# Weight remainders, softmax row maxima and gate functions on other engines, in a two-group encoder layer on Trainium2

## The chip, the cores and the metric

The kernel runs on one core of one Trainium2 chip. Five engines of that core work beside each other, each with its own instruction stream that it takes in order: TensorE (PE, matrix products; PEld is its loading of the stationary operand), VectorE (DVE), ScalarE (ACT), GpSimd (POOL) and SyncE (SP), which here issues every DMA. Matrix products land in PSUM banks, which have to be emptied by VectorE or ScalarE before they can be used again. The metric is the device time of one execution in microseconds; lower is better.

## The reference

One encoder layer is applied to two request groups (1024 tokens by 1024 channels each, float32) that share all weights:

```
mod = silu(c) @ w_ada + b_ada             -> shift, scale, gate
h   = rms_norm(x, norm_g) * (1 + scale) + shift
qa, ka, va, za, qb, kb, vb, zb, ga, gb = split(h @ w_in)
oa  = gqa_attention(rope(rms(qa)), rope(rms(ka)), va) * silu(za)
ob  = rms_norm(diff_attention(...qb, kb, vb, lam), subln_g) * (1 - lam_init) * silu(zb)
merged = sigmoid(ga) * (oa @ w_proj_a) + sigmoid(gb) * (ob @ w_proj_b)
y   = x + gate * (merged @ w_out)
```

Branch A has 8 query heads and 2 key heads of 64; branch B has 4 heads, each with two softmax maps of 1024 by 1024 whose weighted difference is applied to the values. za and zb go through SiLU, ga and gb through a sigmoid.

## The kernel before

**Arithmetic.** Most products are made in three passes: each float32 operand is split into a rounded part (format fp32r) and a remainder, and the products high by high, high by low and low by high are added in one PSUM bank. The rounded part is an ACT copy, the remainder a subtraction. `load_w` (L188) fetches a weight block of 1024 by 256 in four staging tiles `st` (three buffers); `split_w` (L176) rounds each on ACT (L179) and subtracts on POOL, or, in the stages where `alone[0]` is true, on DVE for every second tile (L181). `load_w_proj` (L215) does the same for the two projection matrices, always on POOL (L223).

**One group.** `head` projects keys, values and the first queries of branch A (`kva_gen`, `qa_gen`). Then six attention phases follow, one for each half of A's heads and one for each head of B (`attention`, L869). A step of `scores` (L743) calls `softmax_unit` (L727): four products fill a two-bank score tile `s` (two such tiles exist), DVE reduces the row maximum (L736) and multiplies it by the row's scale `rs`, a column of 128 numbers (L737), and ACT takes the exponential with that scale and bias (L738) into a tile `p` (four buffers). `flip` transposes `p` on DVE in blocks of 32 (L771) and four DMAs put it into `q` (L776); ACT and DVE split it (L784, L785) and PE multiplies by the values (L796, L797, or L836 for B).

**Filling.** PE is kept busy between attention steps by projections for the next phase (L514) and by "z pieces" (`z_gen`, L692). There are 48 of them for each group: 12 blocks of 256 columns (za, zb, then ga and gb by turns), four pieces each. A piece is 24 products into one bank (L703), which ACT copies into the single tile `ev` (L709) and a DMA stores to DRAM (L712). For the first two blocks (za; `SILU = 2`) that copy is a SiLU; the other blocks are stored raw. How many pieces lie in the head and in each phase stands in `Z_HEAD` and `Z_SHARE` (their sixth number is not used); the rest goes into the last phase. How the streams are interleaved is set by `weave` (L72) from `ATT_W`, `IN_A` and `Z_A`, by numbers set by hand.

**End of a group.** `gated_gen` (L909) reads attention outputs and z back from DRAM, takes SiLU of z where it was stored raw (L931), multiplies (L936 for A, L942 for B, then L946 by the row factors) and splits (L947, L948). `merge_gen` (L953) projects each branch (L976), reads a pair of ga or gb tiles into `gg` (L966), takes their sigmoid on ACT (L967, 128 by 1024), and DVE multiplies the product in PSUM by it (L987 for A, L982 for B, which then adds A's part, L983). 16 of these merge pieces belong to A, `16 - TAIL` of them run beside the last attention phase. `out_gen` is the output projection (L1005, L1010).

**Order on the engines.** The program order comes from `weave`. The tile framework then orders each engine's instructions by a simulated timeline with priorities; attention steps are issued at high priority (L886). Every DMA is issued in order on SP.

**At the start**, `start` (L339) makes SiLU of the conditioning vector (L340), and products with `w_ada` make shift and scale; `gate_gen` (L445) makes the gate later.

Of the kernel before, what the change touches and what calls it, by code (L numbers as in the profile page):

```python
# [12 lines left out]
F32 = mybir.dt.float32  # L13
F32R = mybir.dt.float32r
AF = mybir.ActivationFunctionType
ALU = mybir.AluOpType
# [9 lines left out]
HD = 64  # L26
# [5 lines left out]
C_GA, C_GB = 3328, 4352  # L32
# [2 lines left out]


Z_SHARE = (
    (7, 19, 5, 3, 3, 4),
    (9, 14, 7, 3, 2, 6),
)  # L40
Z_HEAD = (6, 6)
Z_HEAD_A = (-0.4, -0.45)
ATT_W = (
    (1.07, 0.837, 1.1, 0.95, 1.07, 1.52),
    (1.15, 1.354, 1.035, 1.15, 0.85, 1.069),
)
IN_A = (
    (0.1, 0.05, 0.2, 0.05, 0.15, 0.1),
    (0.1, -0.05, 0.45, 0.15, 0.15, 0.65),
)  # L50
Z_A = (
    (0.1, 0.0, 0.4, 0.0, 0.0, 0.0),
    (0.15, 0.05, 0.35, 0.15, -0.1, -0.1),
)
LAST_ATT, LAST_FILL = (44, 26)
GATED_A = -0.3
TAIL = 6
TAIL_A = 0.3
LAG = 2

SILU = 2

CUTS = (3, 6)

# [26 lines left out]
def kernel(ctx: ExitStack, tc: tile.TileContext, t: dict):  # L91
    nc = tc.nc
# [83 lines left out]
    def split_w(w, q, st):  # L176
        wh = w[:, q * 2 : q * 2 + 2, 0, :]
        wl = w[:, q * 2 : q * 2 + 2, 1, :]
        nc.scalar.activation(wh, st, AF.Copy)  # L179
        e = nc.vector if alone[0] and q % 2 else nc.gpsimd  # L180
        e.tensor_tensor(out=wl, in0=st, in1=wh.bitcast(F32), op=ALU.subtract)  # L181

    def split_early(what):
        w, sts = what
# [30 lines left out]
    def load_w_proj(br, half):  # L215

        w = wpool.tile([P, 4, 2, 512], F32R, tag="w", name=nm("w"))
        mat = t["w_proj_b" if br else "w_proj_a"][0]
        for c in range(4):
            st = spool.tile([P, 512], F32, tag="st", name=nm("st"))  # L220
            dma(st, mat[c * P : (c + 1) * P, half * 512 : (half + 1) * 512])
            nc.scalar.activation(w[:, c, 0, :], st, AF.Copy)
            nc.gpsimd.tensor_tensor(out=w[:, c, 1, :], in0=st, in1=w[:, c, 0, :].bitcast(F32), op=ALU.subtract)  # L223
        return w


# [183 lines left out]
    def load_tables_B():  # L410
        for dst, src in ((cosB, "cosB"), (sinB, "sinB")):
            for a in range(2):
                dma(dst[:, a], t[src].rearrange("(n p) d -> p n d", p=P))
        for i, src in enumerate(("qn_b", "kn_b")):
            dma(gB[:, i, :], t[src][0].partition_broadcast(P))
        nc.vector.tensor_scalar(out=gB[:, 0, :], in0=gB[:, 0, :], scalar1=SC, scalar2=None, op0=ALU.mult)
        for a in range(2):
            by_q(cosB[:, a], sinB[:, a], gB[:, a], 8)

        nc.vector.tensor_tensor(out=gB[:, 0, 16:], in0=gB[:, 0, 16:], in1=gB[:, 1, 16:], op=ALU.mult)  # L420

# [12 lines left out]
        dma(subg, t["subln_g"].rearrange("o e -> e o"))  # L434
        nc.vector.tensor_scalar(out=subg, in0=subg, scalar1=(1.0 - LAM_INIT) * math.sqrt(2 * HD), scalar2=None, op0=ALU.mult)

    def load_tables_A(st):

# [6 lines left out]
    def gate_gen():  # L445
        for half in range(2):
            acc = gbank()[:2]
            for k in range(NCH):
                st = spool.tile([P, 512], F32, tag="st", name=nm("st"))
                col = 2 * D + half * 512  # L450
                dma(st, w_ada[k * P : (k + 1) * P, col : col + 512])
                nc.tensor.matmul(acc, cT[:, k], st, start=(k == 0), stop=(k == NCH - 1))
                if k % 2:
                    yield 1
            row = rtile()[:2]
            nc.vector.tensor_copy(row, acc)
            ps = gbank()[:, :8].rearrange("p (c g) -> p c g", g=2)
            for c in range(4):
                nc.tensor.transpose(ps[:, c, :], row[:, c * P : (c + 1) * P], ident[:2, :2])
            cs = slice(half * 4, half * 4 + 4)  # L460
            nc.vector.tensor_tensor(
                out=gatec[:, cs], in0=ps, in1=bcol[:, 2, cs].unsqueeze(2).to_broadcast([P, 4, 2]), op=ALU.add
            )


    def ht_gen(g, ht):
# [222 lines left out]
            yield 1  # L689


    def z_gen(ht, col, dst, i0, fn=AF.Copy):  # L692
        w = load_w(w_cols(w_in, (col, 256)))
        for hf in range(2):
            for e in range(2):
# [10 lines left out]
                        )  # L706
                        k += 1
                ev = mtile("ev", [P, 512], bufs=1)
                nc.scalar.activation(ev, ps, fn)  # L709
# [17 lines left out]
    def softmax_unit(q, rs, sw, k, pt, su):  # L727
# [6 lines left out]
            nc.tensor.matmul(s[:, sl], q, k[:, sl], start=True, stop=False)  # L734
            nc.tensor.matmul(s[:, sl], sw, k[:, sl], start=False, stop=True)  # L735
        nc.vector.tensor_reduce(out=m, in_=s, axis=AX.X, op=ALU.max, negate=True)  # L736
        nc.vector.tensor_tensor(out=m, in0=m, in1=rs, op=ALU.mult)  # L737
        nc.scalar.activation(  # L738
            pt.rearrange("p (j c a) -> p j c a", j=4, c=8), s.rearrange("p (c a j) -> p j c a", c=8, j=4),
            AF.Exp, scale=rs, bias=m, accum_out=su,  # L740
# [168 lines left out]
    def gated_gen(st, i, hf, oT):  # L909

        if i == 0 and hf == 0:
            su = st["suA"].rearrange("p j n -> p (j n)")
            nc.vector.reciprocal(su, su)
            ps = fbank()[:64, :P]
            nc.tensor.transpose(ps, su, ident)
            row = rtile()[:64, :P]
            nc.scalar.activation(row, ps, AF.Copy)
            dma(st["rA"], row)
        rA = st["rA"].rearrange("(j h n) p -> j h (n p)", j=8, h=2)
        u = utile().rearrange("p (c s n) -> p c s n", c=2, s=2)  # L920
# [4 lines left out]
        for c in range(2):  # L925
# [1 line left out]
            o, z = (os_[c], zs_[c]) if i == 3 else (rtile(), rtile())  # L927
            dma(o, st["od"][e][hf])
            dma(z, st["zd"][(e, hf)])
            if i >= SILU:  # L930
                nc.scalar.activation(z, z, AF.Silu)  # L931
            if e < 4:
                rb = mtile("tab", [P, 512])
                for a in range(2):
# [18 lines left out]
    def merge_gen(st, br, oT, mT):  # L953

        for half in range(2):
            w = load_w_proj(br, half)
            for hf in range(2):
# [3 lines left out]
                for d in range(4):  # L961
                    dt_ = half * 4 + d
                    if d % 2 == 0:
                        gg = ptile().rearrange("p (a n) -> p a n", a=2)
                        for a in range(2):
                            dma(gg[:, a, :], st["gbd" if br else "gad"][(dt_ + a, hf)])  # L966
                        nc.scalar.activation(gg, gg, AF.Sigmoid)  # L967
                        if br:
                            mT[hf].append(utile().rearrange("p (c s n) -> p c s n", c=2, s=2))
                    g = gg[:, d % 2, :]  # L970
# [8 lines left out]
                            k += 1  # L979
                    if br:  # L980
                        mh, ml = (mT[hf][dt_ // 2][:, d % 2, i, :] for i in range(2))
                        nc.vector.tensor_tensor(out=g, in0=ps, in1=g, op=ALU.mult)  # L982
                        nc.vector.tensor_tensor(out=g, in0=g, in1=md[:, d], op=ALU.add)  # L983
                        nc.scalar.activation(mh, g, AF.Copy)
                        nc.vector.tensor_tensor(out=ml, in0=g, in1=mh.bitcast(F32), op=ALU.subtract)
                    else:
                        nc.vector.tensor_tensor(out=md[:, d], in0=ps, in1=g, op=ALU.mult)  # L987
                    yield 1

    def out_gen(g, mT):  # L990
# [95 lines left out]

    def z_item(st, i):
        ht = st["ht"]
        fn = AF.Silu if i < SILU else AF.Copy
        if i < 2:  # L1090
            return z_gen(ht, C_ZA + i * 256, st["zd"], i * 2, fn)
        if i < 4:
            return z_gen(ht, C_ZB + (i - 2) * 256, st["zd"], i * 2, fn)
        i -= 4
        if i % 2 == 0:
            return z_gen(ht, C_GA + i * 128, st["gad"], i)
        return z_gen(ht, C_GB + (i - 1) * 128, st["gbd"], i - 1)

    states = [new_state(0), new_state(1)]
    late = start(states[0]["ht"])  # L1100
# [111 lines left out]
```

## Time and profile before

| | |
|---|---|
| time, median of 3 runs | 1973.39 us (1972.16 to 1973.81) |
| span of the profiled execution, first to last instruction | 1971.9 us |
| TensorE (PE) busy | 1901.8 us, 96% |
| weight loads (PEld) busy, beside PE | 1619.1 us, 82% |
| VectorE (DVE) busy | 1353.0 us, 69% |
| ScalarE (ACT) busy | 1012.0 us, 51% |
| GpSimd (POOL) busy | 680.9 us, 35% |
| data moved by DMA | 295 MB, 150 GB/s on average |

The profiled execution has no time of its own beside its span. The three timed runs lie 0.3 to 1.9 us above that span, the median 1.5 us; that is what lies around it. A row of a group of instructions reads: line, engine, operation, out<-in with the program's tile names (buffer numbers left out), shapes, count, then busy time and the mean duration in ns, then the idle time of that engine just before, and what ended it. A row of waits reads: who waited <- for whom: total us, how many times, longest. A row of the timeline begins with start and duration in us, and ends, in brackets, with the idle time before it. A row of windows gives the busy time of each engine in a stretch, its granted TensorE clock and its share of DMA time.

### The profile page before, as it was taken

How to read it: one execution, taken by the hardware profiler on the slowest of the kernel's cores; microseconds unless marked ns; L12 is line 12 of the kernel's file. 1: busy time of each engine (PE TensorE's matmuls, PEld its weight loads, DVE VectorE, ACT ScalarE, POOL GpSimd, SP SyncE). 2: the span in 40 equal slices, each digit the busy share in tenths (PEclk: the TensorE clock that was granted, in tenths of full speed). 3: DMA queues.
4: the chain of work that ended last, by engine and by line, in shares of the span. 5: the costliest groups of instructions: out<-in, count | busy, mean ns of one | idle time of the engine just before them, and what ended most of it. 6: DMA issues, size and time to landing. Idle time of an engine off the chain costs nothing. (4 is left out here: it accounts for less than half of the span.)

```text
span 1971.9 us, 30870 instructions
## 1 busy us (share of the span) xinstructions
PE 1901.8 (96%) x10466; PEld 1619.1 (82%) x10466; DVE 1353.0 (69%) x2165; ACT 1012.0 (51%) x1920; POOL 680.9 (35%) x958
## 2 busy tenths in 40 slices
PE   8999999999989999999999999999999999998999
PEld 3888888888878985778889788888888889776887
DVE  4658876786888577757465598768878766776641
ACT  4447655565655353464323576556666444447410
POOL 2363511442446251322235344114444426322210
PEclk9899999999999999999999999999999999999999
DMA  9125545556454345865641355555555334478431
GB/s 315 33 89 149 144 139 149 158 156 174 127 144 111 89 117 173 272 234 179 222 151 44 115 144 167 148 149 157 156 152 161 98 102 119 120 222 267 166 102 75
DMA packets 271614, 295.26 MB, mean 150 GB/s; under 512 B 37856, under 2 KB 220256, under 8 KB 271456
## 3 DMA queue, kind: packets, MB, share of 16 engines
q1 hardware_dynamic: 271456, 293.28, 50.1%
q8 instruction: 84, 1.38, 0.3%
q14 instruction: 74, 0.61, 0.1%
HBM read 133.72 MB, written 42.01 MB: 89 GB/s over the span
## 5 line engine op out<-in xcount | busy, mean ns | idle before, releaser
L703 PE MATMUL f<-u,w 128*128 128x512 f32 x2184 | 561.3, 395 | 3.0 <-ACT w L179 1.3
L514 PE MATMUL f<-w,u 128*128 128x256 f32 x3456 | 489.6, 286 | 5.2 <-ACT ev L709 2.7
L514 PEld LDWEIGHTS f<-w,u 128*128 128x128 f32 x3456 | 460.7, 192 | 26.8 <-ACT ev L709 3.7
L703 PEld LDWEIGHTS f<-u,w 128*128 128x128 f32 x2184 | 396.8, 189 | 78.1 <-ACT w L179 1.8
L181 POOL TENSOR_TENSOR w<-st,w 128x512 fp32r<-128x512 f32 x166 | 227.8, 1391 | 463.2 <-ACT w L179 412.9
L736 DVE TENSOR_REDUCE m<-s 128x1 f32<-128x1024 f32 x256 | 310.2, 1217 | 55.1 <-PE s L735 52.0
L771 DVE STREAM_TRANSPOSE p<-p 128x1024 f32<-128x1024 f32 x192 | 238.0, 1241 | 112.8 <-ACT p L738 110.2
L785 DVE TENSOR_TENSOR q<-q,hi 128x512 fp32r<-128x512 f32 x256 | 193.9, 774 | 47.9 <-ACT hi L784 46.4
L738 ACT ACTIVATE p<-s,m,rsB 128x1024 f32<-128x1024 f32 x128 | 154.0, 1204 | 135.0 <-DVE m L737 103.3
L738 ACT ACTIVATE p<-s,m,rsA 128x1024 f32<-128x1024 f32 x128 | 153.8, 1202 | 128.1 <-DMA q<-p 95.8
L735 PE MATMUL s<-u,sw 128*128 128x512 f32 x512 | 205.0, 401 | 0.0
L784 ACT ACTIVATE hi<-q 128x512 fp32r<-128x512 f32 x256 | 153.2, 624 | 78.2 <-DMA q<-p 50.2
L179 ACT ACTIVATE w<-st 128x512 fp32r<-128x512 f32 x196 | 114.2, 626 | 101.9 <-DMA st<-in_w_in_dram 46.6
L976 PE MATMUL f<-u,w 128*128 128x512 f32 x552 | 136.4, 400 | 11.3 <-ACT ev L709 4.1
L796 PE MATMUL a<-hi,u 128*128 128x256 f32 x512 | 132.0, 284 | 4.8 <-DVE oo L813 3.1
L976 PEld LDWEIGHTS f<-u,w 128*128 128x128 f32 x552 | 104.8, 192 | 35.3 <-DVE u L987 4.6
L836 PE MATMUL a<-q,u 128*128 128x256 f32 x512 | 125.9, 385 | 5.6 <-DMA q<-p 1.9
L797 PE MATMUL a<-q,u 128*128 128x256 f32 x512 | 129.8, 287 | 0.5 <-DVE q L785 0.4
L734 PE MATMUL s<-u 128*128 128x512 f32 x256 | 109.5, 428 | 7.9 <-ACT p L738 4.0
L734 PE MATMUL s<-u,u 128*128 128x512 f32 x256 | 103.3, 404 | 13.8 <-ACT p L738 9.0
L836 PEld LDWEIGHTS a<-q,u 128*128 128x128 f32 x512 | 95.9, 193 | 21.6 <-issue 2.9
L735 PEld LDWEIGHTS s<-u,sw 128*128 128x128 f32 x512 | 97.4, 190 | 15.5
(186 smaller groups left out, 2639.1 us busy)
## 6 DMA issues: line engine op xcount, KB each, us to landing
q<-p SPq DMA_DIRECT2D x768, 128.0 KB, 2.6
st<-in_w_in_dram SPq DMA_DIRECT2D x132, 256.0 KB, 3.0
zd<-ev SPq DMA_DIRECT2D x96, 256.0 KB, 2.2
sw<-u SPq DMA_DIRECT2D x256, 64.0 KB, 2.0
p<-zd SPq DMA_DIRECT2D x64, 256.0 KB, 3.8
u<-in_w_ada_dram SPq DMA_DIRECT2D x8, 1024.0 KB, 10.4
st<-in_w_in_dram SPq DMA_DIRECT2D x64, 128.0 KB, 2.7
st<-in_w_out_dram SPq DMA_DIRECT2D x32, 256.0 KB, 3.2
```

Source lines behind the costliest of these rows:

```text
L181: e.tensor_tensor(out=wl, in0=st, in1=wh.bitcast(F32), op=ALU.subtract)
L514: nc.tensor.matmul(ps, lt[c][:, sl], w[:, c, wi, :], start=(k == 0), stop=(k == 23))
L703: nc.tensor.matmul(ps, w[:, c, wi, e * P : (e + 1) * P], rt[c], start=(k == 0), stop=(k == 23),)
L734: nc.tensor.matmul(s[:, sl], q, k[:, sl], start=True, stop=False)
L735: nc.tensor.matmul(s[:, sl], sw, k[:, sl], start=False, stop=True)
L736: nc.vector.tensor_reduce(out=m, in_=s, axis=AX.X, op=ALU.max, negate=True)
L738: nc.scalar.activation(pt.rearrange("p (j c a) -> p j c a", j=4, c=8), s.rearrange("p (c a j) -> p j c a", c=8, j=4), AF.Exp, scale=rs, bi ...
L771: nc.vector.transpose(pt, pt)
L784: nc.scalar.activation(th, tl.bitcast(F32), AF.Copy)
L785: nc.vector.tensor_tensor(out=tl, in0=tl.bitcast(F32), in1=th.bitcast(F32), op=ALU.subtract)
L836: nc.tensor.matmul(acc, u["v"][:, k], pT[:, k], start=(k == 0), stop=(k == 7))
L976: nc.tensor.matmul(ps, w[:, c, wi, d * P : (d + 1) * P], o[:, oi, :], start=(k == 0), stop=(k == 11))
```

## The change

- **Weight remainders:** all of them are subtracted by DVE instead of POOL (`split_w`, `load_w_proj`).
- **Row maxima:** the multiplication of the row maximum by the row scale becomes an ACT copy with a scale.
- **Gates:** SiLU and sigmoid are written with tanh: sigmoid(x) = (1 + tanh(x/2)) / 2. The factors 1/2 go into constants: into `subg` for B, into the row factors (L917) for A, into `gatec` for the merge. Each z piece is emptied by a tanh; for za and zb, DVE then makes (1 + tanh) times the bank and writes `ev`. The SiLU of `gated_gen` and the sigmoid of `merge_gen` go; DVE's multiplications in the merge become (1 + g) times the bank. The conditioning vector's SiLU is made the same way.
- **Pieces:** numbers of `Z_SHARE`, `Z_HEAD`, `ATT_W`, `IN_A`, `Z_A` and `TAIL` are changed.

```
-    (7, 19, 5, 3, 3, 4),
+    (7, 19, 6, 3, 2, 4),
     (9, 14, 7, 3, 2, 6),
-Z_HEAD = (6, 6)
+Z_HEAD = (6, 5)
 ATT_W = (
-    (1.07, 0.837, 1.1, 0.95, 1.07, 1.52),
-    (1.15, 1.354, 1.035, 1.15, 0.85, 1.069),
+    (1.07, 0.933, 1.1, 0.95, 1.129, 1.52),
+    (1.15, 1.354, 1.035, 1.196, 0.85, 1.069),
 IN_A = (
-    (0.1, 0.05, 0.2, 0.05, 0.15, 0.1),
-    (0.1, -0.05, 0.45, 0.15, 0.15, 0.65),
+    (0.1, -0.05, 0.2, 0.05, 0.15, 0.1),
+    (0.1, -0.05, 0.45, 0.25, 0.15, 0.65),
 Z_A = (
-    (0.1, 0.0, 0.4, 0.0, 0.0, 0.0),
-    (0.15, 0.05, 0.35, 0.15, -0.1, -0.1),
+    (0.1, 0.0, 0.4, -0.05, -0.2, 0.0),
+    (0.15, 0.05, 0.35, 0.15, -0.3, -0.2),
-TAIL = 6
+TAIL = 5
-SILU = 2
...
     def split_w(w, q, st):
         nc.scalar.activation(wh, st, AF.Copy)
-        e = nc.vector if alone[0] and q % 2 else nc.gpsimd
-        e.tensor_tensor(out=wl, in0=st, in1=wh.bitcast(F32), op=ALU.subtract)
+        nc.vector.tensor_tensor(out=wl, in0=st, in1=wh.bitcast(F32), op=ALU.subtract)
...
     def load_w_proj(br, half):
-            nc.gpsimd.tensor_tensor(out=w[:, c, 1, :], in0=st, in1=w[:, c, 0, :].bitcast(F32), op=ALU.subtract)
+            nc.vector.tensor_tensor(out=w[:, c, 1, :], in0=st, in1=w[:, c, 0, :].bitcast(F32), op=ALU.subtract)
...
     def start(ht):
-        nc.scalar.activation(cT, ccol, AF.Silu)
+        nc.scalar.activation(cT, ccol, AF.Tanh, scale=0.5)
+        nc.vector.scalar_tensor_tensor(out=cT, in0=cT, scalar=1.0, in1=ccol, op0=ALU.add, op1=ALU.mult)
+        nc.vector.tensor_scalar(out=cT, in0=cT, scalar1=0.5, scalar2=None, op0=ALU.mult)
...
     def gate_gen():
+            nc.vector.tensor_scalar(out=gatec[:, cs], in0=gatec[:, cs], scalar1=0.5, scalar2=None, op0=ALU.mult)
...
     def z_gen(ht, col, dst, i0, gated):
                 ev = mtile("ev", [P, 512], bufs=1)
-                nc.scalar.activation(ev, ps, fn)
+                nc.scalar.activation(ev, ps, AF.Tanh, scale=0.5)
+                if gated:
+                    nc.vector.scalar_tensor_tensor(out=ev, in0=ev, scalar=1.0, in1=ps, op0=ALU.add, op1=ALU.mult)
...
     def softmax_unit(q, rs, sw, k, pt, su):
-        nc.vector.tensor_tensor(out=m, in0=m, in1=rs, op=ALU.mult)
+        nc.scalar.activation(m, m, AF.Copy, scale=rs)
...
     def gated_gen(st, i, hf, oT):
-            nc.scalar.activation(row, ps, AF.Copy)
+            nc.scalar.activation(row, ps, AF.Copy, scale=0.5)
...
-            if i >= SILU:
-                nc.scalar.activation(z, z, AF.Silu)
...
     def merge_gen(st, br, oT, mT):
-                        nc.scalar.activation(gg, gg, AF.Sigmoid)
...
-                        nc.vector.tensor_tensor(out=g, in0=ps, in1=g, op=ALU.mult)
+                        nc.vector.scalar_tensor_tensor(out=g, in0=g, scalar=1.0, in1=ps, op0=ALU.add, op1=ALU.mult)
...
-                        nc.vector.tensor_tensor(out=md[:, d], in0=ps, in1=g, op=ALU.mult)
+                        nc.vector.scalar_tensor_tensor(
+                            out=md[:, d], in0=g, scalar=1.0, in1=ps, op0=ALU.add, op1=ALU.mult
+                        )
```

More of the change, by code (lines that the diff above doesn't have):

```diff
@@ L37 @@
 Z_SHARE = (
-    (7, 19, 5, 3, 3, 4),
+    (7, 19, 6, 3, 2, 4),
     (9, 14, 7, 3, 2, 6),
 )
-Z_HEAD = (6, 6)
+Z_HEAD = (6, 5)
 Z_HEAD_A = (-0.4, -0.45)
 ATT_W = (
-    (1.07, 0.837, 1.1, 0.95, 1.07, 1.52),
-    (1.15, 1.354, 1.035, 1.15, 0.85, 1.069),
+    (1.07, 0.933, 1.1, 0.95, 1.129, 1.52),
+    (1.15, 1.354, 1.035, 1.196, 0.85, 1.069),
 )
 IN_A = (
-    (0.1, 0.05, 0.2, 0.05, 0.15, 0.1),
-    (0.1, -0.05, 0.45, 0.15, 0.15, 0.65),
+    (0.1, -0.05, 0.2, 0.05, 0.15, 0.1),
+    (0.1, -0.05, 0.45, 0.25, 0.15, 0.65),
 )
 Z_A = (
-    (0.1, 0.0, 0.4, 0.0, 0.0, 0.0),
-    (0.15, 0.05, 0.35, 0.15, -0.1, -0.1),
-)
-LAST_ATT, LAST_FILL = (44, 26)
+    (0.1, 0.0, 0.4, -0.05, -0.2, 0.0),
+    (0.15, 0.05, 0.35, 0.15, -0.3, -0.2),
+)
+LAST_ATT = 44
+LAST_FILL = 26
 GATED_A = -0.3
-TAIL = 6
+TAIL = 5
 TAIL_A = 0.3
 LAG = 2
-SILU = 2
 CUTS = (3, 6)
@@ L434, in load_tables_B @@
         dma(subg, t["subln_g"].rearrange("o e -> e o"))
-        nc.vector.tensor_scalar(out=subg, in0=subg, scalar1=(1.0 - LAM_INIT) * math.sqrt(2 * HD), scalar2=None, op0=ALU.mult)
+        nc.vector.tensor_scalar(out=subg, in0=subg, scalar1=0.5 * (1.0 - LAM_INIT) * math.sqrt(2 * HD), scalar2=None, op0=ALU.mult)
     def load_tables_A(st):
@@ L689, in vb_gen, with z_gen @@
             yield 1
-    def z_gen(ht, col, dst, i0, fn=AF.Copy):
+    def z_gen(ht, col, dst, i0, gated):
         w = load_w(w_cols(w_in, (col, 256)))
@@ L1088, in z_item @@
         ht = st["ht"]
-        fn = AF.Silu if i < SILU else AF.Copy
         if i < 2:
-            return z_gen(ht, C_ZA + i * 256, st["zd"], i * 2, fn)
+            return z_gen(ht, C_ZA + i * 256, st["zd"], i * 2, True)
         if i < 4:
-            return z_gen(ht, C_ZB + (i - 2) * 256, st["zd"], i * 2, fn)
+            return z_gen(ht, C_ZB + (i - 2) * 256, st["zd"], i * 2, True)
         i -= 4
         if i % 2 == 0:
-            return z_gen(ht, C_GA + i * 128, st["gad"], i)
-        return z_gen(ht, C_GB + (i - 1) * 128, st["gbd"], i - 1)
+            return z_gen(ht, C_GA + i * 128, st["gad"], i, False)
+        return z_gen(ht, C_GB + (i - 1) * 128, st["gbd"], i - 1, False)
     states = [new_state(0), new_state(1)]
```

## The prediction

> **What bounds the kernel now.** I read the page's first part, then the busy times by stretch, then what TensorE waited for, and last the timeline at its longest waits.
>
> ```profile
> PE 1901.8 (96%) x10466; PEld 1619.1 (82%) x10466; DVE 1353.0 (69%) x2165; ACT 1012.0 (51%) x1920; POOL 680.9 (35%) x958
> ```
>
> TensorE is the bound: all that a change which leaves its products alone can win is its idle time, 1971.9 - 1901.8 = 70 us, and what its clock loses. The change has the same products, so the question is only which of these stalls go and which come.
>
> ```profile
> core 0: us, PE busy (x) PEld busy (x) DVE busy (x) ACT busy (x) POOL busy (x), PEclk, DMA share, GB/s
> ...
> 1095.00:1150.00 55.00, 50.17 (x258) 41.71 (x256) 34.99 (x47) 35.93 (x58) 18.73 (x20) 0.97 0.51 145
> 820.00:850.00 30.00, 25.89 (x112) 21.25 (x113) 19.55 (x29) 18.59 (x27) 6.69 (x9) 0.94 0.93 298
> 1775.00:1805.00 30.00, 23.07 (x98) 17.72 (x97) 22.60 (x36) 22.39 (x27) 4.50 (x6) 0.94 0.86 283
> 150.00:820.00 670.00, 650.82 (x3734) 559.08 (x3733) 501.76 (x768) 372.70 (x719) 249.34 (x374) 0.99 0.52 147
> ```
>
> The first three rows are the second group's first softmaxes and the two merges: 4.8, 4.1 and 6.9 us of idle in 115 us, while the first group's long attention stretch loses 19.2 us in 670. In the three short ones the granted clock falls too: 0.03 x 55 = 1.65 us, and 0.06 x 30 = 1.8 us twice. In the attention DVE is busy 75% of the time, ACT 56%.
>
> ```profile
> PE s L734 <- ACT p L738: 13.0, 15, 1.6
> ...
> PE f L976 <- ACT ev L709: 4.1, 1, 4.1
> ...
> PE f L514 <- ACT ev L709: 2.7, 2, 2.3
> ```
>
> The first row is the attention's own limit: the next score products wait for one of two score tiles, which an exponential has yet to empty. The second is a merge's longest wait, the third that of the projections for z banks.
>
> **The change part by part.**
>
> *Sigmoid and SiLU leave the merges.* The timeline around the first group's wait, and then the second's:
>
> ```profile
> 837.63 1.04 ACT L967 ACTIVATE p<-p 128x1024 f32<-128x1024 f32 x1
> ...
> 838.76 1.28 ACT L931 ACT_TABLE_LOAD   x1
> ...
> 840.05 0.63 ACT L931 ACTIVATE row<-row 128x512 f32<-128x512 f32 x1
> 840.59 0.58 ACT L709 ACTIVATE ev<-f 128x512 f32<-128x512 f32 x1
> ...
> 841.22 4.63 PE L976 MATMUL f<-u,w 128*128 128x512 f32 x12 [4.11 <-ACT ev L709]
> ```
>
> ```profile
> 1782.96 1.06 ACT L967 ACTIVATE p<-p 128x1024 f32<-128x1024 f32 x1
> ...
> 1784.05 1.29 DVE L987 TENSOR_TENSOR u<-f,p 128x512 f32<-128x512 f32 x2 [0.98 <-ACT p L967]
> ...
> 1784.80 5.78 PE L976 MATMUL f<-u,w 128*128 128x512 f32 x24 [2.61 <-DVE u L987]
> ...
> 1791.49 0.75 DVE L942 SCALAR_TENSOR_TENSOR row<-row,subg,row 128x512 f32<-128x512 f32 x1 [3.49 <-ACT row L931]
> ...
> 1793.11 4.50 PE L976 MATMUL f<-u,w 128*128 128x512 f32 x12 [2.54 <-DVE row L946]
> ```
>
> At 841 PE waits 4.11 us for a bank whose emptying (L709) stands behind a sigmoid (1.04), a table load (1.28) and a SiLU (0.63). Without them 2.95 us go and 1.16 stay. At 1784 the product waits for DVE, which waited 0.98 us for a sigmoid: 0.98 goes. At 1793 DVE waited 3.49 us for a SiLU, more than PE's 2.54, so all 2.54 go. That is 6.5 us, and the two dips of the clock (1.8 us each) go with them if what remains is short: 10.1 us. What is late next is the DMA that brings the gate tiles, at a DMA share of 0.93 and 0.86; that is the first rival.
>
> *No change of table between the first softmaxes.*
>
> ```profile
> L967 ACT ACT_TABLE_LOAD x10 | 12.8, 1283 | 8.3 <-DMA p<-zd 8.1
> L738 ACT ACT_TABLE_LOAD x9 | 11.5, 1283 | 2.6 <-DVE m L737 2.5
> L931 ACT ACT_TABLE_LOAD x9 | 11.5, 1283 | 2.7 <-DMA row<-zd 2.6
> L709 ACT ACT_TABLE_LOAD x8 | 10.3, 1283 | 7.3 <-PE s L703 3.7 <-issue 3.6
> ```
>
> Only the lines that use SiLU, a sigmoid or the exponential after one of them load a table; copies, squares and exponentials run without. The loads at L709 and eight of those at L738 come from the za pieces that fall between exponentials. Of 1095 to 1150 the view of waits gives this:
>
> ```profile
> PE s L734 <- ACT p L738: 2.8, 2, 1.6
> ```
>
> Both waits have a load of 1.28 us ahead of the exponential; I count 2.5 of the 2.8 us, and the dip of 1.65: 4.1 us. This needs tanh and the exponential to share a table, which no run here shows. The Trainium skill says in "ScalarE: Activation LUTs", section "Table sets: the hidden batching unit", that the set of exp also holds tanh; by it no load but the first is left and the sum stands, and without it the last rival holds.
>
> *Row maxima on ACT.*
>
> ```profile
> L737 DVE TENSOR_TENSOR m<-m,rsA 128x1 f32<-128x1 f32 x128 | 30.1, 238 | 2.1
> ...
> L737 DVE TENSOR_TENSOR m<-m,rsB 128x1 f32<-128x1 f32 x128 | 25.9, 209 | 1.7
> ...
> L377 ACT ACTIVATE u<-u,modc 128x512 f32<-128x512 f32 x8 | 5.6, 713 | 0.5 <-DVE u L374 0.5
> ...
> L528 ACT ACTIVATE row<-row 128x128 f32<-128x128 f32 x16 | 4.9, 308 | 0.0
> ...
> L378 ACT ACTIVATE u<-u 128x512 fp32r<-128x512 f32 x8 | 4.8, 617 | 0.0
> ```
>
> The trace has no ACT copy of one column. From 512 to 128 elements a copy falls from 617 to 308 ns, 0.80 ns an element, so one element is about 206; a column as operand adds 713 - 617 = 96: an estimate of 0.30 us, between 0.2 and 0.4. DVE loses 256 multiplications, 56 us; ACT gains 256 x 0.30 = 77 us and loses 46 us of loads, 32 sigmoids of 1.06 (34 us) and 16 SiLU of 0.63 (10 us). The direct step grows by about 0.08 us. But on DVE it also queues:
>
> ```profile
> 789.23 2.30 DVE L736 TENSOR_REDUCE m<-s 128x1 f32<-128x1024 f32 x2
> ...
> 792.53 0.20 DVE L737 TENSOR_TENSOR m<-m,rsB 128x1 f32<-128x1 f32 x2
> ```
>
> Here the second maximum was there at 791.53 and was scaled 1.0 us later, behind other DVE work; on ACT the exponential would follow at once. 10.2 us of the 13.0 of waits on exponentials are left after the part above. Bounds: all 10.2 go, or each of 13 waits grows by 0.2 (+2.6). I take half, -5.1, since an ACT that is 56% busy queues less than a DVE at 75%. A rule speaks against this edit: the Trainium skill, "ScalarE: Activation LUTs", section "Rules for kernel authors", gives multiplications to VectorE and not to ScalarE. By it each link is slower by some 0.1 us and this term would be +1 to +2 us instead of -5.1; the L737 rows, whose 238 ns already hold delays, are why I don't follow it.
>
> *Remainders on DVE.*
>
> ```profile
> L181 POOL TENSOR_TENSOR w<-st,w 128x512 fp32r<-128x512 f32 x166 | 227.8, 1391 | 463.2 <-ACT w L179 412.9 <-DMA od<-oo 28.4 <-DVE q L1010 18.2
> ...
> L785 DVE TENSOR_TENSOR q<-q,hi 128x512 fp32r<-128x512 f32 x256 | 193.9, 774 | 47.9 <-ACT hi L784 46.4
> ...
> L181 DVE TENSOR_TENSOR w<-st,w 128x512 fp32r<-128x512 f32 x30 | 31.5, 1051 | 27.4 <-ACT w L179 27.3
> ...
> L379 DVE TENSOR_TENSOR u<-u,u 128x512 fp32r<-128x512 f32 x8 | 5.2, 682 | 0.0
> ```
>
> The same subtraction of 128x512 takes 682 ns where POOL is quiet (L379), 774 in the attention and 1051 beside POOL (L181): DVE and POOL hold each other up. 166 subtractions, and the 32 of `load_w_proj` (2 groups, 2 branches, 2 halves, 4 tiles), at 0.68 are 135 us on DVE. 32 za and zb pieces add a product with two operations, at 0.75 as L942 in the timeline above: 24 us. L737 takes off 56, and POOL's shorter list takes off some of 256 x 0.09 + 30 x 0.37 = 34 us of delay, half by my estimate: 17. DVE goes from 1353 to about 1440 us, 73%. PE's waits on DVE are few (the rows above), so I put +2 us, from -3 (delays gone) to the slower rival.
>
> *z banks are held longer.* A gated bank is free after the tanh and a DVE product, 0.75 us and a hop more. Two waits of L514 on L709 (2.7 us) become 0.75 longer each: +1.5 us, nothing at best, and 24 us (32 x 0.75) if every piece were waited for.
>
> *Pieces.* One piece moves from phase 4 to phase 2 of the first group, one from the second group's head to its end, one merge piece to before the attention's end. 24 products take 5.78 us (the row at 1784.80), so each move is under 6 us of filling, against stalls of a few us on either side: 0, from -6 to +6. The new start (tanh and two small DVE steps in place of a SiLU) lies before PE's wait for the first weights: 0.
>
> **Sum:** -10.1 - 4.1 - 5.1 + 2 + 1.5 = -15.8 us on the span: 1956.1. The median lies 1.5 us above the span, which makes 1957.6; I say **1957.5**, with 1945 to 1970 as this case's own range.
>
> **The rivals.**
>
> *Stalls only change their cause.* The merges then wait for the gate tiles' DMAs:
>
> ```profile
> ACT p L967 <- DMA p<-zd: 33.0, 16, 5.9
> ```
>
> 16 waits of 2 us on that DMA stand against the 6.5 us of PE. If they take the 10.1 us back, -4.1 - 5.1 + 3.5 and a little for displaced filling leave about 1970, within the error of no change.
>
> *More goes than I count.* The matmul in flight hides part of each wait, so the weight loader's view is longer:
>
> ```profile
> PEld s L734 <- ACT p L738: 28.8, 28, 3.8
> ```
>
> If the shorter link clears nearly all of them (28.8 - 2.8 = 26 us instead of 5.1), the sum is -37 and the time 1937. For it: the queueing seen at 792. Against it: the exponential also waits for its output buffers, whose DMAs don't change.
>
> *Slower: DVE is blocked by its new subtractions.* Each waits for an ACT copy that waits for a staging DMA, and all that DVE has queued behind it waits too: reductions, transposes, splits, and so the exponentials and PE. The row of L181 on DVE has the price: 27.3 us of waiting in 30, 0.91 each. The place is the attention after the heads:
>
> ```profile
> 1150.00:1250.00 100.00, 98.22 (x561) 85.47 (x561) 85.41 (x123) 64.28 (x124) 37.02 (x41) 1.00 0.55 153
> ```
>
> If 12 subtractions fall into such 100 us, DVE's 85.4 become 85.4 + 12 x 0.68 - 5 = 88.6, and 12 x 0.91 of waits make 99.5: just full. Above 0.95 us a subtraction PE pays for all of it. The page's second part shows how much of the span is like that:
>
> ```profile
> DVE  4658876786888577757465598768878766776641
> ```
>
> 11 of 40 slices have an 8 or a 9, 540 us. At 1.4 us a subtraction the excess is 12 x 0.45 = 5.4 us per 100, 29 in all: 1957.6 + 29 = 1987; at 1.9 us it is 2019. Against it: the scheduler can put the subtraction where its data are there, and POOL's 413 us of waiting show that nobody waited for these remainders.
>
> *Not what it says: tanh needs its own table.* 84 z pieces of both groups lie outside the heads; each would cost two loads, 168 x 1.28 = 215 us of ACT. 16 such loads cost PE 2.8 + 1.65 us now, 0.28 each: +47 us, about 2004.
>
> **How the numbers follow.** My forecast has 0.42, more than counted 0.22, causes that only change 0.12, blocked DVE 0.20, tanh's table 0.03. A measurement of this kernel tells 0.2% (4 us) from no change. Faster by more: most of the first two and a little of the third, 0.66. Within: 0.10. Slower: 0.24. The range goes from 1926 (the larger gain, 1937, with the pieces' 6 us and 5 of DVE's delays) to 1988 (the blocked cases up to 1.4 us, half of them), and leaves out under 2 in 10.
>
> **What would show it.** ACT_TABLE_LOAD down to one or two; no PE wait over 2 us at L976, the clock at 1.00 around both merges; PE's waits on L738 under 9 us; L785 under 730 ns; DVE at 71 to 75%. DVE waiting for L179 over 200 us with PE waits on DVE behind it would make the slower rival right; the merges' waits ended by DMA, the first.

## The result, and the profile after

The kernel after takes 1938.05 us (median of 4 runs, 1933.24 to 1945.97) against 1973.6 us: 0.983 of before (95% interval 0.980 to 0.985). 35.5 us went, where the prediction had 16. The direction and the range held; the size was off by more than two.

The profiled execution is the fastest of the four: its span went from 1971.9 to 1931.5 us, by 40.4. The first row of its page, then its mean granted clock, then that of the kernel before:

```profile
PE 1881.2 (97%) x10466; PEld 1610.0 (83%) x10466; DVE 1397.3 (72%) x2145; ACT 991.7 (51%) x2091; POOL 414.7 (21%) x758
```

```profile
core 0: 1931.5 us, clock 0.995
```

```profile
core 0: 1971.9 us, clock 0.990
```

The same 10466 products kept TensorE busy 20.6 us less (1901.8 to 1881.2), and its idle time fell from 70.1 to 50.3 us. So half of the gain of this execution is in time that the profile had called busy.

The clock is part of that: 1% of 1971.9 us was 19.7 us of clock lost, 0.5% of 1931.5 is 9.7, so some 10 us by this estimate. Six of them lie in the first 100 us, ahead of the attention, where the granted clock lies anywhere from 0.90 to 0.97 in the profiles of the kernels below. The kernel before, then after:

```profile
0.00:100.00 100.00, 87.67 (x420) 58.22 (x421) 54.75 (x134) 46.50 (x102) 30.68 (x44) 0.91 0.51 172
```

```profile
0.00:100.00 100.00, 85.81 (x443) 56.83 (x444) 58.36 (x149) 44.34 (x101) 23.77 (x44) 0.97 0.54 182
```

Not all of these 10 us belong to the median. The other three runs had clocks of 0.992, 0.992 and 0.988 and took 5 to 13 us longer, and span times clock is 1921 to 1922 us in all four: between them the time follows the clock. At the median's 0.992 some 15 us of clock are lost instead of 10, so 4 to 5 of the 35.5 us came by the clock and about 30 at an equal clock.

The other 10.6 us of busy time do not come from shorter products. The durations of all PE groups add up to 2387.6 us before and 2379.5 after (products overlap, so the sum is larger than the busy time), 8 us less, about what the clock gives. So the products lie closer together. That would fit short gaps which the profile's modelled ends cover; no run here shows such a gap itself.

Where it went, by stretches: the attention of each group, then its merge and gates. The kernel before:

```profile
141.00:821.00 680.00, 660.82 (x3771) 567.05 (x3770) 508.87 (x776) 377.63 (x726) 251.25 (x376) 0.99 0.52 147
1096.00:1781.00 685.00, 663.78 (x3812) 578.38 (x3811) 517.68 (x783) 386.01 (x740) 254.12 (x382) 1.00 0.52 146
821.00:933.00 112.00, 107.89 (x492) 89.40 (x492) 72.22 (x111) 60.27 (x83) 21.54 (x20) 0.98 0.66 220
1781.00:1881.00 100.00, 93.05 (x417) 75.99 (x416) 66.58 (x99) 57.59 (x75) 19.31 (x16) 0.98 0.59 196
```

The kernel after:

```profile
139.00:804.00 665.00, 654.98 (x3780) 565.29 (x3779) 525.21 (x733) 403.87 (x848) 159.85 (x307) 1.00 0.54 150
1075.00:1744.00 669.00, 652.23 (x3779) 574.23 (x3778) 525.26 (x736) 403.26 (x851) 158.13 (x306) 0.99 0.53 146
804.00:910.00 106.00, 104.42 (x481) 85.97 (x480) 75.18 (x119) 28.80 (x50) 3.58 (x5) 1.00 0.69 232
1744.00:1840.00 96.00, 94.96 (x435) 77.87 (x434) 70.97 (x113) 26.48 (x47) 5.22 (x6) 1.00 0.64 214
```

The merges' idle time fell from 4.1 + 7.0 to 1.6 + 1.0 us and their clock went from 0.98 to 1.00. The attention's idle time fell from 19.2 + 21.2 to 10.0 + 16.8, although VectorE is busier there (75 to 79%). By their lengths, 31 of the 40.4 us lie in the two attention stretches (1365 to 1334 us; about 4 of them are 24 products that moved out, at 0.175 us each) and 10 in the merges (212 to 202). The second group's first softmaxes, 1095 to 1150 before, have no idle time left and a clock of 1.00. The largest loss that remains is a stretch later in that group's attention, with 11.9 us of idle and a clock of 0.93. Both rows are of the kernel after:

```profile
1074.00:1130.00 56.00, 56.00 (x329) 49.41 (x327) 47.88 (x63) 35.83 (x75) 14.00 (x20) 1.00 0.52 144
1395.00:1500.00 105.00, 93.08 (x503) 79.09 (x502) 84.94 (x118) 66.01 (x138) 19.79 (x42) 0.93 0.50 137
```

The waits of TensorE that answer to those shown before, and the weight loader's:

```profile
PE s L737 <- ACT p L741: 6.4, 5, 2.0
...
PE f L515 <- DVE ev L712: 3.1, 1, 3.1
...
PE s L737 <- DVE ev L712: 2.8, 1, 2.8
...
PE f L976 <- DVE u L987: 1.3, 2, 0.7
```

```profile
PEld s L737 <- ACT p L741: 12.5, 10, 3.2
```

Waits on exponentials halved (13.0 to 6.4, by the weight loader 28.8 to 12.5). The longest wait at L976 is 0.7 us instead of 4.1. The two rows with `ev` are new: banks held for the product of the gates. The groups that the change touches:

```profile
L788 DVE TENSOR_TENSOR q<-q,hi 128x512 fp32r<-128x512 f32 x256 | 171.5, 690 | 34.3 <-ACT hi L787 32.3 <-DMA sw<-u 0.5
...
L179 DVE TENSOR_TENSOR w<-st,w 128x512 fp32r<-128x512 f32 x196 | 132.8, 706 | 34.2 <-ACT w L178 33.1
...
L740 ACT ACTIVATE m<-m,rsB 128x1 f32<-128x1 f32 x128 | 37.3, 291 | 113.9 <-DVE m L739 113.6
L740 ACT ACTIVATE m<-m,rsA 128x1 f32<-128x1 f32 x128 | 37.1, 290 | 70.2 <-DVE m L739 69.7
...
L338 ACT ACT_TABLE_LOAD x1 | 1.3, 1283 | 0.7 <-PEq L1192 0.7
```

Of the 36 table loads shown before none is left; one remains, at the start. The split of the softmax (L788, L785 before) takes 690 ns instead of 774. The row maximum takes 290 ns on ACT.

### The profile page after: what moved, and what is told of

The parts are those of the page before. It is cut to its first block, busy times and chain, and to the rows that moved or that the text cites. A ratio compares the mean times of both kernels' runs of the same rounds, so it can differ in the third digit from the quotient of the medians.

```text
span 1931.5 us, 30797 instructions
## 1 busy us (share of the span) xinstructions
PE 1881.2 (97%) x10466; PEld 1610.0 (83%) x10466; DVE 1397.3 (72%) x2145; ACT 991.7 (51%) x2091; POOL 414.7 (21%) x758
## 4 chain that ended last, share of the span: by engine, by line
PE 81%; DVE 7%; DMA 5%; issue 2%; ACT 2%; SPq 1%; POOL 1%; DVEq 0%; ACTq 0%; POOLq 0%
PE f L704 22%; PE f L515 19%; PE f L1007 5%; PE s L737 5%; PE a L839 5%; PE s L738 5%; PE f L976 4%; PE s L1007 4%; PE a L800 3%; PE a L799 3%; PE s L976 2%; DMA q<-p 2%; DVE m L739 2%; DVE p L774 1%; PE f L298 1%
## 5 line engine op out<-in xcount | busy, mean ns | idle before, releaser
L739 DVE TENSOR_REDUCE m<-s 128x1 f32<-128x1024 f32 x256 | 311.0, 1217 | 51.3 <-PE s L738 48.4
L774 DVE STREAM_TRANSPOSE p<-p 128x1024 f32<-128x1024 f32 x192 | 238.3, 1241 | 92.7 <-ACT p L741 89.3
L788 DVE TENSOR_TENSOR q<-q,hi 128x512 fp32r<-128x512 f32 x256 | 171.5, 690 | 34.3 <-ACT hi L787 32.3
L741 ACT ACTIVATE p<-s,m,rsA 128x1024 f32<-128x1024 f32 x128 | 153.8, 1202 | 71.4 <-DMA q<-p 69.6
L178 ACT ACTIVATE w<-st 128x512 fp32r<-128x512 f32 x196 | 114.4, 625 | 99.2 <-DMA st<-in_w_in_dram 42.4
L741 ACT ACTIVATE p<-s,m,rsB 128x1024 f32<-128x1024 f32 x128 | 154.3, 1205 | 6.5 <-DMA q<-p 1.9
L179 DVE TENSOR_TENSOR w<-st,w 128x512 fp32r<-128x512 f32 x196 | 132.8, 706 | 34.2 <-ACT w L178 33.1
L658 POOL TENSOR_TENSOR row<-row,gB 128x96 f32<-128x96 f32 x64 | 33.8, 528 | 485.7 <-ACT row L529 474.1
L976 PE MATMUL f<-u,w 128*128 128x512 f32 x540 | 130.5, 393 | 1.3 <-DVE u L987 1.3
L976 PEld LDWEIGHTS f<-u,w 128*128 128x128 f32 x540 | 100.5, 188 | 23.0 <-DVE u L987 2.3
L737 PE MATMUL s<-u 128*128 128x512 f32 x256 | 108.3, 424 | 3.3 <-ACT p L741 3.2
L737 PE MATMUL s<-u,u 128*128 128x512 f32 x256 | 102.4, 400 | 8.5 <-ACT p L741 3.1
```

The lines of the kernel that those rows point to most:

```text
L741: nc.scalar.activation(pt.rearrange("p (j c a) -> p j c a", j=4, c=8), s.rearrange("p (c a j) -> p j c a", c=8, j=4), AF.Exp, scale=rs, bi ...
L774: nc.vector.transpose(pt, pt)
L976: nc.tensor.matmul(ps, w[:, c, wi, d * P : (d + 1) * P], o[:, oi, :], start=(k == 0), stop=(k == 11))
```

## The experiments

All ratios are to the kernel before on the same chip, with 95% intervals. The groups of runs were taken on different chips; the kernel before took 1971.9 to 1974.5 us on them, so differences in us between groups are good to some 3 us.

**One part alone.** Four kernels, each the kernel before with one part of the diff shown above.

Gates alone (the diff's hunks in `start`, `gate_gen`, `z_gen`, `gated_gen`, `merge_gen`, `subg`):

```
-                nc.scalar.activation(ev, ps, fn)
+                nc.scalar.activation(ev, ps, AF.Tanh, scale=0.5)
...
-                        nc.scalar.activation(gg, gg, AF.Sigmoid)
```

> The kernel before with the tanh gates alone (z banks emptied by tanh, no SiLU, no sigmoid in the merges; the other parts and all numbers of the phases as before). Theory of the prediction (gates): the two merges lose 10 us of stalls, the second group's first softmaxes 4, held banks give 1.5 back: -12 us, 0.994 of before. Rival (VectorE is freed: ports and row maxima carry the gain): -5 to -12 in the merges alone, nothing in the attention stretches. Rival (numbers of the phases): -12 or less.

Measured: 1978.22 us, 1.002 (1.001 to 1.004). Slower, and yet the merges did what was predicted. Their rows:

```profile
827.50:937.00 109.50, 107.04 (x491) 87.75 (x489) 74.88 (x110) 28.81 (x50) 23.23 (x20) 1.00 0.69 226
1792.00:1886.00 94.00, 91.40 (x419) 75.38 (x418) 68.91 (x100) 24.27 (x41) 19.46 (x16) 1.00 0.63 211
```

Idle 2.5 + 2.6 us instead of 4.1 + 7.0, at a clock of 1.00. The loss came elsewhere: by the bounds of these rows, the stretch ahead of the first merge is 6.5 us longer than before and the one between the merges 7 us.

Row maxima alone:

```
-        nc.vector.tensor_tensor(out=m, in0=m, in1=rs, op=ALU.mult)
+        nc.scalar.activation(m, m, AF.Copy, scale=rs)
```

> The kernel before with the row maxima scaled on ScalarE alone. Theory of the prediction: -5 us (0.997), half of PE's waits on exponentials. Rival (the softmax link was the attention's limit, the prediction took too little of it): -15 us or more, and PE's idle time before L734 that ends at L738 falls by more than half. Rival (ports): within 4 us of before, because the link only changes its engine while remainders on GpSimd still hold VectorE up.

Measured: 1977.01 us, 1.003 (1.001 to 1.004). The weight loader's waits on exponentials did not fall (28.8 before), and those of TensorE's products rose from 13.0 to 23.5 us:

```profile
PEld s L734 <- ACT p L738: 30.6, 24, 3.6
```

Remainders alone:

```
-        e = nc.vector if alone[0] and q % 2 else nc.gpsimd
-        e.tensor_tensor(out=wl, in0=st, in1=wh.bitcast(F32), op=ALU.subtract)
+        nc.vector.tensor_tensor(out=wl, in0=st, in1=wh.bitcast(F32), op=ALU.subtract)
```

> The kernel before with the weight remainders on VectorE alone. Theory of the prediction: +2 us (within 0.2%). Rival (ports): VectorE's subtraction at L785 falls from 774 to below 700 ns, its small L737 from 238 and 209 to about 150, and the time falls by 10 to 20 us although VectorE has more to do. Rival (blocked VectorE): slower by 10 us or more, waits of VectorE on L179 above 150 us.

Measured: 1991.21 us, 1.009 (1.007 to 1.011). The durations are those of the rival with the ports, the time is not. Its groups, and its waits:

```profile
L784 DVE TENSOR_TENSOR q<-q,hi 128x512 fp32r<-128x512 f32 x256 | 172.4, 690 | 23.7 <-ACT hi L783 22.6
...
L736 DVE TENSOR_TENSOR m<-m,rsA 128x1 f32<-128x1 f32 x128 | 19.8, 157 | 1.5
L736 DVE TENSOR_TENSOR m<-m,rsB 128x1 f32<-128x1 f32 x128 | 19.7, 157 | 1.5
```

```profile
DVE w L180 <- ACT w L179: 35.0, 29, 3.3
```

```profile
PEld s L733 <- ACT p L737: 21.2, 17, 6.7
```

The split falls to 690 ns and the row maximum from 238 and 209 to 157 ns, all by taking work off GpSimd. VectorE waits only 35 us for 196 remainders: blocked VectorE is not what made this kernel slow. The weight loader's waits on exponentials fell to 21.2 us. None of the other parts lowered them alone (28.0 with the gates, 30.6 with the row maxima, 32.1 with the numbers).

Numbers of the phases alone:

```
-    (7, 19, 5, 3, 3, 4),
+    (7, 19, 6, 3, 2, 4),
...
-TAIL = 6
+TAIL = 5
```

> The kernel before with the new numbers of the phases alone. Theory of the prediction: 0, from -6 to +6 us. Rival (the numbers carry the surplus of the gain): -10 to -20 us already here. Rival (the numbers fit only the other parts): slower here, by up to 10 us, and slower again when the old numbers are put into the kernel after.

Measured: 1994.05 us, 1.011 (1.009 to 1.013). The four parts alone sum to +46 us, together they give -36: they cannot be read one by one.

**One part taken back** from the kernel after, the same hunks reversed.

> The kernel after with SiLU and sigmoid as before (raw z blocks, gates in the merges). Theory of the prediction, corrected by the first four runs (the gates' part is sound, about 9 us in the merges, and the other attention stages move by some 10 us with any new order): slower than the kernel after by 10 to 20 us, 7 to 12 of them in the two merges. Rival (the numbers of the phases fit only the whole): slower by 20 to 40, most of it in the attention.

Measured: 1964.04 us, 0.994 (0.992 to 0.996): 26 us slower than the kernel after, more than the theory's 20 and in the range of the rival. By the bounds of the rows below 11 us of them lie in the merges, whose stalls are back:

```profile
PE f L976 <- ACT ev L709: 5.6, 1, 5.6
PE f L976 <- DVE u L987: 1.7, 1, 1.7
```

```profile
815.00:927.00 112.00, 106.39 (x480) 87.87 (x479) 75.26 (x121) 63.87 (x88) 4.51 (x5) 0.97 0.67 220
1770.00:1871.00 101.00, 96.71 (x437) 79.07 (x436) 68.33 (x109) 56.79 (x78) 5.39 (x6) 0.98 0.62 203
```

> The kernel after with the row maxima scaled on VectorE again. Theory (row maxima on ScalarE matter once VectorE has more to do): slower than the kernel after by 5 to 15 us, PE's waits on exponentials above 12 us. Rival (numbers fit only the whole): slower by 15 to 40. Rival (row maxima are worth nothing): within 5 us.

Measured: 1970.29 us, 0.997 (0.996 to 0.998), 32 us slower than the kernel after, as much as the rival with the fit had. The waits on exponentials are above 12 us, as the theory had them, only if a merge product is counted in: 9.9 us at L737 and 4.0 at L976.

> The kernel after with the weight remainders on GpSimd again. Rival (ports carry the surplus): slower by 15 us or more, with the subtraction at L788 back above 750 ns. Theory of the prediction (remainders cost VectorE a little): within 5 us of the kernel after, or faster.

Measured: 1971.29 us, 0.998 (0.997 to 1.000), 33 us slower. The split is at 746 ns (the expectation had above 750), and waits on exponentials are back:

```profile
L789 DVE TENSOR_TENSOR q<-q,hi 128x512 fp32r<-128x512 f32 x256 | 186.0, 746 | 50.2 <-ACT hi L788 48.3 <-DMA zd<-ev 0.8
```

```profile
PEld s L738 <- ACT p L742: 24.7, 18, 5.2
```

> The kernel after with the old numbers of the phases. Theory of the prediction (parts -16 us, numbers 0): 1955 to 1962 us. Rival (the numbers fitted to the whole carry the surplus): 1960 to 1985, and the losses against the kernel after lie in the attention stretches, not in the merges. Rival (the parts alone carry all of the gain): 1936 to 1945.

Measured: 1980.49 us, 1.0035 (1.002 to 1.005): with all three parts but the old numbers the kernel is slower than before. The time lies in the range of the rival with the fitted numbers, but not only the attention loses: the waits at the merges' products are 7.7 us, against 1.3 in the kernel after.

So each single step from either kernel costs: +4 to +21 us from the kernel before, +26 to +42 from the kernel after. That is what fitted numbers look like: a single undone part may also undo the fit. The next kernels shift the numbers without changing anything else.

**Shifted numbers.** All twelve numbers of `ATT_W` times 1.01 or 0.99, in both kernels:

```
-    (1.07, 0.933, 1.1, 0.95, 1.129, 1.52),
-    (1.15, 1.354, 1.035, 1.196, 0.85, 1.069),
+    (1.0807, 0.9423, 1.111, 0.9595, 1.1403, 1.5352),
+    (1.1615, 1.3675, 1.0454, 1.208, 0.8585, 1.0797),
```

> The kernel before with all twelve numbers of ATT_W times 1.01, a change that moves nothing but the order of the filling by a step here and there. Theory (numbers are a fit: a small shift of any tuned kernel costs it some 20 us, and what the parts are worth shows between shifted kernels): 1975 to 1995. Rival (the time follows the numbers smoothly): within 5 us of the kernel before.

Measured: 2000.64 us, 1.014 (1.012 to 1.016), more than the fit theory had.

> The kernel before with all twelve numbers of ATT_W times 0.99. Theory (fit): 1975 to 1995. Rival (smooth): within 5 us of the kernel before.

Measured: 1986.9 us, 1.007 (1.005 to 1.009).

> The kernel after with all twelve numbers of ATT_W times 1.01. Theory (fit): 1955 to 1975, 15 to 35 us slower than the kernel after; if the mean of the shifted kernels after is some 15 us below that of the shifted kernels before, the parts are worth what the prediction said, and the rest of the 36 us is the fit. Rival (smooth): within 5 us of the kernel after.

Measured: 1958.36 us, 0.993 (0.991 to 0.995).

> The kernel after with all twelve numbers of ATT_W times 0.99. Theory (fit): 1955 to 1975. Rival (smooth): within 5 us of the kernel after.

Measured: 1947.52 us, 0.987 (0.985 to 0.989), less than the fit theory had.

A shift of 1%, which changes the order of the work and none of it, costs 15 to 29 us before (1972.0 us on that chip) and 9 to 20 after: the smooth rival falls. But the shifted kernels after lie 42 and 39 us below the shifted kernels before, not 15. So the whole change, parts and new numbers, is worth more than twice the forecast at shifted numbers too, and my theory that the surplus is a fit to the exact numbers falls.

What the three parts are worth without the new numbers does not follow from this. With the old numbers they cost 7 us (1973.6 to 1980.5), with the new ones they gain 56 (1994.1 to 1938.1), and when each kernel has the other's numbers the difference is 14 us (1994.1 and 1980.5), near the forecast. The parts and the numbers depend on each other, and how much the new numbers carry beside the parts stays open: the new parts with shifted old numbers were not run, nor the old parts with shifted new ones.

**Which part?** The same shifts in kernels that lack one part.

> The kernel after with SiLU and sigmoid as before and ATT_W times 1.01. Theory (the gates are worth the 13 us of the prediction): with its sister at 0.99 and the unshifted 1964, a mean of 1961 to 1971, with 7 to 12 us of stalls more in the merges than in the kernels after. Rival (the gates carry more): above 1975.

> The same with ATT_W times 0.99: the expectation is of the mean with its sister kernel; a single value can lie 10 us off the mean.

Measured: 1965.77 us (0.997, 0.996 to 0.999) and 1975.03 us (1.0025, 1.001 to 1.004); with the unshifted 1964.04 a mean of 1968.3, within the theory's 1961 to 1971. The waits at the merges' products are 7.8 and 8.3 us, some 7 more than in the shifted kernels after.

> The kernel after with row maxima on VectorE again and ATT_W times 1.01. Theory (parts add up, row maxima are worth 15 us or more): with its sister at 0.99 and the unshifted 1970, a mean of 1965 to 1980. Rival (the prediction's 5 us): a mean of 1955 to 1962. Rival (fit of the numbers): a mean like the shifted kernels after, 1953.

> The same with ATT_W times 0.99: the expectation is of the mean with its sister kernel; a single value can lie 10 us off the mean.

Measured: 1959.51 us (0.993, 0.990 to 0.997) and 1979.21 us (1.003, 1.0015 to 1.005); mean with the unshifted one 1969.7, within the theory's 1965 to 1980.

> The kernel after with remainders on GpSimd again and ATT_W times 1.01. Theory (VectorE freed of GpSimd is worth some 10 us or more): with its sister and the unshifted 1971, a mean of 1960 to 1980. Rival (the prediction: remainders cost 2 us): a mean of 1945 to 1955.

> The same with ATT_W times 0.99: the expectation is of the mean with its sister kernel; a single value can lie 10 us off the mean.

Measured: 1980.3 us (1.005, 1.003 to 1.007) and 1970.07 us (0.999, 0.998 to 1.001); mean 1973.9, within the theory's 1960 to 1980.

| numbers not fitted to the kernel (three kernels each) | us | mean | PEld waits of score products on exponentials, us |
|---|---|---|---|
| parts before: up, down, new numbers | 2000.6, 1986.9, 1994.1 | 1993.9 | 31.7, 27.9, 32.1 |
| parts after: up, down, old numbers | 1958.4, 1947.5, 1980.5 | 1962.1 | 18.3, 16.7, 19.9 |
| after without gates | 1964.0, 1965.8, 1975.0 | 1968.3 | 23.3, 23.3, 22.5 |
| after without row maxima on ACT | 1970.3, 1959.5, 1979.2 | 1969.7 | 19.5, 14.6, 16.1 |
| after without remainders on VectorE | 1971.3, 1980.3, 1970.1 | 1973.9 | 24.7, 30.0, 22.5 |

The times within a row scatter by 10 us (standard deviation, pooled over the rows), so a mean of three is good to some 6 us and a difference of two means to 8. All parts together, 32 us, stand out of that. One part taken back, 6, 8 and 12 us, does not. The rows do not hold the same numbers, though: the second has a kernel with the old ones where the last three have the new ones unshifted. Over the two shifts alone the kernels after have a mean of 1953, and a part taken back costs 17 (gates), 16 (row maxima) and 22 us (remainders), each with an error of 10. That adds up to 56, and all parts and numbers together are worth 41 there. So the parts do not add up, and **time does not settle the split.**

The waits do in part. They depend less on the fit: with the parts before they are 27.9 to 32.1 us, whatever the numbers. Without the remainders on VectorE they rise from between 16.7 and 19.9 to between 22.5 and 30.0, and without the gates to 23. Without the row maxima on ACT they stay where they were (14.6 to 19.5), but there a merge product waits for an exponential too, 4.2 to 4.6 us in each of the three kernels, which no kernel with all parts shows. With it the sums are 19.2 to 23.7. The rows for row maxima taken back, and for the gates taken back:

```profile
PEld s L737 <- ACT p L741: 19.5, 16, 4.1
PEld s L976 <- ACT p L741: 4.2, 1, 4.2
```

```profile
PEld s L734 <- ACT p L738: 23.3, 17, 4.5
```

## Why the prediction was right in direction and wrong in size

**The step that failed** is the sum for the attention beyond its first softmaxes: row maxima -5.1, remainders +2, z banks +1.5 and pieces 0, together -1.6 us. In the profiled executions the attention stretches became 31 us shorter; without some 4 us of products that moved and 6.4 us in the first softmaxes about 20 us are left, 9 of them idle time, where the prediction had 1.6. The merges (10 us shorter) and, by the medians, the clock (4 to 5 us against 5.25) came out as counted. What the runs show in place of that step: the waits on exponentials halved, and of the parts tried alone only the remainders lowered them (28.8 to 21.2), not the row maxima (30.6), to which the prediction gave the gain. How the 20 us divide stays open.

- **Gates in the merges: right.** -10.1 us were counted (6.5 of idle, 3.6 of clock). Measured: 8.4 us of idle and a clock from 0.98 to 1.00 over 112 and 100 us, 4.2. It is there in the kernel with gates alone, and gone when they are taken back. Not by the gates alone, though: with SiLU and sigmoid still in the merges the waits of their products are between 2.2 us (remainders alone) and 15.6 (the kernel before at 0.99), and with tanh between 0.3 and 7.7. The order of the work decides as well. The first rival, the DMA of the gate tiles in place of the sigmoid, did not come.
- **Table loads: right.** The 36 are gone, and the first softmaxes gained 4.8 us of idle and 1.65 of clock, against 4.1 counted. The trace agrees with what the Trainium skill says in "ScalarE: Activation LUTs", section "Table sets: the hidden batching unit": tanh and the exponential need no change of table here, and the rival with 168 loads falls.
- **Price of a row maximum on ACT: right** (0.30 us estimated, 0.29 measured). **Its worth: not shown.** It was given -5.1 us for shorter waits on exponentials. Alone it left the weight loader's waits at 30.6 us, and taken back they are 14.6 to 19.5, or 19.2 to 23.7 with the merge product; the time, 8 us by three kernels, is within the scatter. The queueing seen at 792 us was real for one softmax; no run shows that it was worth half of the waits. The rule of the Trainium skill that gives multiplications to VectorE ("ScalarE: Activation LUTs", section "Rules for kernel authors") is neither borne out nor refuted by these runs.
- **Remainders on VectorE: the sign of the step was probably wrong.** It was given +2 us with 17 us of delays taken off VectorE. The delays that went are larger: 256 x (774 - 690) = 21.5 us at the split, and the row maximum fell by 52 to 81 ns where it stayed on VectorE. Where those delays lie was not followed: some are on the link from score tile to exponential, whose waits rise from between 16.7 and 19.9 us to between 22.5 and 30.0 when GpSimd has the remainders. By time the sign is not settled: alone the part costs 18 us, and taken back it costs 12 with an error of 8, or 22 with one of 10. The slower rival is refuted by its own sign: 34.8 us of waits on L178 in 196 remainders is 0.18 us each, not 0.91 or more.

```profile
DVE w L179 <- ACT w L178: 34.8, 32, 2.5
```

- **z banks: the sign was right, the size too small.** +1.5 us were counted. The waits for `ev` that were 2.7 us at the projections are 3.1, and a score product waits 2.8 us for a bank that the new product holds: +3.2.
- **Pieces: the bound was wrong.** "Under 6 us of filling, against stalls of a few us on either side" counted what moves. What matters is which product stands where in all twelve phases: the numbers alone cost 21 us before, and taking them back 42 us after. What they are worth in the whole is not shown; if it is near nothing, that is the sum of two large things, a broken fit and a new one, and not what the step argued.
- **The bound of the whole, and the unit of the terms: wrong.** "All that a change which leaves its products alone can win is its idle time, 1971.9 - 1901.8 = 70 us, and what its clock loses" took a busy TensorE to be at work. The terms were read from idle rows and from two-digit clocks: 10.6 us of idle and 5.25 of clock. Measured in the profiled execution were 19.8 of idle, 10 of clock (4 to 5 in the median) and 10.6 in busy time beside the clock. The weight loader's row for the same waits on exponentials, 28.8 us against 13.0 in that of the products, hinted at it, and the prediction had it only in a rival. That rival (1937 us) had the time right, but for a reason that is at most half right: it laid all the shorter waits on the row maxima. To that extent its time is luck. The Trainium skill says, in "Trainium Kernel Development and Optimization", section "Performance Expectations", that matmul busy time is a bad measure of distance to the limit; the busy time that the same products lost beside the clock agrees.
- The signs named in advance all came (one table load, no merge wait over 2 us, clock 1.00, 6.4 us on L741, 690 ns, 72%). They tested mechanisms and not the size, and so did not tell 16 from 36 us. The five chances of the prediction add up to 0.99.

What stays open: how the gain divides between the parts and the new numbers, and how the remainders and the gates act together; a part's worth would need each kernel's numbers fitted to it anew. It wasn't tried to keep GpSimd busy without touching VectorE's operands, which would have shown the delay apart from the order of the work.

## What to carry to other kernels

In a kernel whose order is fitted by hand, an edit taken alone can lose the fit first (here a shift of 1% cost 9 to 29 us); compare both versions at shifted numbers before judging it, and at each other's. A sound edit can look worthless until the order is fitted again. Where TensorE is 96% busy, read the weight loader's waits and the clock beside its idle time: in the profiled execution half of what was won had stood under busy. Compare clocks over several executions, because one profile may have caught a good one. When VectorE and GpSimd work on the same memory, count what each costs the other, and look for the delay on the chain that releases the next product.

## What the runs showed of the hardware that was not expected

A VectorE multiplication of 128 numbers took 238 and 209 ns on average beside GpSimd's remainders and 157 without them, and a subtraction of 128x512 774 against 690: GpSimd's remainders held up even the smallest instruction of VectorE that reads two operands, though no data passed between the two. VectorE's row reductions and transposes, which read one, took 1217 and 1241 ns before and after. Executions of one and the same kernel spread by 0.65% (1933.24 to 1945.97 us), in step with the mean granted clock, 0.995 to 0.988.
